# A sixth seven-product pair in the second half of an out projection

## The chip, the cores and the metric

The kernel runs on one core of a Trainium2 chip. The metric is device microseconds of one execution; times of a kernel are medians of runs on the chip. One more execution was recorded by the hardware profiler, and all rows below come from that one.

## The reference

One layer of an encoder trunk on 256 positions of width 2048, all in float32. The part that matters here is the end of the mixer:

```python
merged = g_a * (y_a @ w_branch[:GM_WIDTH]) + g_b * (y_b @ w_branch[GM_WIDTH:])
return x + merged @ w_out          # 256x2048 @ 2048x2048
```

Ahead of it stand a combined projection of the normed input, a gated MLP branch and neighbourhood attention; behind it a convolutional MLP (up projection, depthwise convolution, down projection) and a last norm.

## The kernel before, in words

**Products.** TensorE multiplies float32 with both operands split into a high and a low part, so every product of two blocks is three matmuls (`triple`, L319 to L321): high by high, low by high, high by low. Weights come from HBM in pieces of 128 rows by 1024 columns (`wraw`), and each piece is split by one ScalarE copy (`whi`, L172) and one VectorE subtraction (`wlo`, L173).

**Steps.** The whole kernel is a list of pieces; step i is TensorE's work on piece i. `begin(i)` first issues the load of piece i + 4 on SP's queue, then the split of piece i + 3, then the tasks that other code registered for step i with `at(i, f)`, in the order of their registration. So the order of every engine's queue is written out by hand, in steps. Attention's steps start at 48 (`g_at[0][1]`), the branch products of the second half of the merge at 160 (`g_m2[0][1]`), the out projection's first half (`g_o[0]`, output columns 0 to 1023) at 176, its second half (`g_o[1]`) at 192, the up projection at 208.

**Seven products.** `wide` and `run_wide` do one half of the out projection: 16 pieces, each one k block of 128 rows by two column halves of 512, against two blocks of 128 positions. A plain step is 4 products. Two neighbouring k blocks make a pair, 8 products, and a pair that is named in `OUT_QUADS` is done with 7, by sums of weight blocks and sums of activation blocks (a Winograd form). Of such a pair the first step has 3 products (into the PSUM banks P[0], C[0][0], C[0][1]) and the second has 4 (P[1], P[3], P[2], C[1][0], in that order). The four P banks run through all seven-product pairs of a half and are then added by VectorE (`ev_sums`); the four C banks hold the plain sums, and are read at the half's end (`ev_out`, L1025). `OUT_ORDER` gives the order of the k blocks: 10, 11, 0, 1, 6, 7, 2, 3, 8, 9, 4, 5 and then 12 to 15, so pair 5 comes first, then pairs 0, 3, 1, 4, 2, then two plain ones. Before, places 1 to 5 of both halves are seven-product pairs.

**Sums of weights.** For most such pairs `weight_sums` (L356 to L366, four VectorE additions) and `weight_sums_split` (L376, L377) make them close ahead of their use. For pairs 3 and 4 they are made much earlier: `split_ahead` (L1299 to L1328) is a job in attention that loads 1 MB of raw weights, makes the four additions (L1310), splits twice (ScalarE L1315, VectorE L1316) and writes four tiles of 512 KB to HBM (L1320); `split_read` (L1270) reads them back on POOL's queue into tiles of `hpool` (pair 3) or of the pool `twice` (pair 4). Of the pair's first piece only one column half is then loaded and split. `OUT_SPLIT` holds the pairs and how many steps ahead of the pair the two reads are issued. Before, the four out jobs and the four gate jobs of attention use SP's queue; out jobs load into `jobs`, most gate jobs into `jobs2`.

**Sums of activations.** `turn_m(j)` turns the merged blocks with TensorE, splits them (`split_pair`, VectorE L538) and for pairs in `OUT_PAIRS` copies them to an `f` tile on ScalarE (L982). `turned_sums` (L341) makes four sums of 128x128 from it (`act_blocks`, L325 to L328) and `act_sums_split` splits them into a tile `s0` to `s4`. `OUT_SUMS` gives the steps, counted from step 160.

**Banks.** `bank()` takes one of eight PSUM banks; a bank is handed out again when what was in it has been read.

Of the kernel before, what the change touches and what calls it, by code (L numbers as in the profile page):

```python
# [8 lines left out]
F32 = mybir.dt.float32  # L9
# [48 lines left out]
GATE_SUMS = ((0, 38, 40, "y4", "y5"), (3, 39, 40, "y6", "y7"))  # L58
GATE_LATE, Y_LATE, TURN_LATE = 7, 44, 2
KEEP_AT = (22, 25, 29)  # L60
OUT_PAIRS = (0, 1, 2, 3, 4)
OUT_SUMS = (1, 3, 6, 9, 13)
OUT_QUADS = ((1, 2, 3, 4, 5),) * 2
OUT_ORDER = ((10, 11, 0, 1, 6, 7, 2, 3, 8, 9, 4, 5, 12, 13, 14, 15),) * 2
OUT_SET = 3
OUT_JOB = (10, (15, 15, 15, 15), (17, 20))
OUT_SPLIT = ({3: (16, 14), 4: (5, 5)}, {3: (12, 10), 4: (12, 10)})
TURN_X2 = (13, 1)
Y_GAP = 224
PAD = 16  # L70
# [10 lines left out]
def trunk_kernel(ctx, tc, x, x_t, vecs, w_in, ln_g, ln_b, w_st, b_s, rpb, w_branch, w_out, w_up, w_down,  # L81
                 norm_final, out):
    nc = tc.nc
# [42 lines left out]
    raw, split_t = {}, {}  # L126
# [64 lines left out]
    def at(i, f):  # L191
        tasks.setdefault(i, []).append(f)
# [130 lines left out]
    def act_blocks(w, a11, a21, a12, a22):  # L323
        s3, n1, p2, s4 = (w[:, n * 128:(n + 1) * 128] for n in range(4))
        nc.vector.tensor_sub(s3, a11, a21)  # L325
        nc.vector.tensor_sub(n1, a22, a21)
        nc.vector.tensor_add(p2, n1, a11)
        nc.vector.tensor_sub(s4, a12, p2)  # L328
# [10 lines left out]
        box["w"] = w  # L339

    def turned_sums(q, box):  # L341
        f, w = mg["f", q], out_sums_room("f", F32)
        act_blocks(w[:, 1], *(f[:, n * 128:(n + 1) * 128] for n in range(4)))
        box["w"] = w

# [225 lines left out]
    def first_room(name, dt):  # L571
        return ypool.tile([128, 2, 512], dt, name=f"y{first_rooms.index('t13' if name == 'f' else name)}")
# [137 lines left out]
    at_pool = {}  # L710
# [193 lines left out]
    mg = {}  # L904
# [59 lines left out]

    def room_f(q):
        if ("f", q) not in mg:
            mg["f", q] = mg["fp"].tile([128, 512], F32, name=f"f{q}")
        return mg["f", q]

    def turn_m(j):  # L970
# [8 lines left out]
        for k2, p in enumerate(ps):  # L979
            k = j * 4 + k2 * 2  # L980
            if k // 2 in OUT_PAIRS:
                nc.scalar.activation(room_f(k // 2), p, AF.Copy)  # L982
# [241 lines left out]
    w_br, w_o, w_u, w_d = w_branch[0], w_out[0], w_up[0], w_down[0]  # L1224
# [3 lines left out]
    def sums_room(name, dt):  # L1228
        return s_room["p"].tile([128, 2, 512], dt, name=name)
# [15 lines left out]
    for n, (q, i, j) in enumerate(X_SUMS):  # L1245
        sum_acts_at(i, j, first_sums[2 * q], lambda q=q: q,
                    lambda name, dt, i=i: first_room("s2" if name == "f" and i < 16 else name, dt), f"s{n}", True)
    g_u = [stationary(w_in2, 0, KD, U0 + j * 512, 512, 1, 0, xt, ev_u(j)) for j in range(2)]
    def g_qk(j):
        return stationary(w_in2, 0, KD, Q0 + j * 256, 256, 2, K0 - Q0, xt, ev_qk(j))  # L1250

    def g_gate(br, j):
        return natural(w_in2, 0, KD, (GA0, GB0)[br] + j * 512, 512, xt, ev_gate(br, j))

    def g_branch(br, j):
        return natural(w_br, br * 1024, 8, j * 512, 512, lambda k: yT[br * 8 + k], ev_branch(br, j))

    g_at = [g_qk(0), g_gate(0, 0), g_qk(1), g_gate(1, 0), g_qk(2), g_gate(0, 1), g_qk(3), g_gate(1, 1),
            g_branch(0, 0), g_branch(0, 1)]
    g_m = [g_branch(1, 0), g_branch(1, 1)]  # L1260
    m_sums = {2 * q: {} for q in OUT_PAIRS}
    g_kept, x_kept = {}, {}
    gate_turn, gate_held = [0], {}

    def split_read(kept, g, tile_of, queue=nc.gpsimd):
        def read(pair, box, n):
            u = box.setdefault("u", [])
            u.append([tile_of(pair, p + n) for p in "hl"])
            for t, src in zip(u[-1], kept[pair, g][n]):
                queue.dma_start(t.bitcast(F32), src)  # L1270
            if len(u) == 2:
                split_sums(box, u)
        return read
# [20 lines left out]
    def out_sums_room(name, dt):  # L1294
        if name in ("s0", "s1", "s2", "s3"):
            return hpool.tile([128, 2, 512], dt, name=out_room[name])
        return sums_room("l24" if name == "f" else name, dt)

    def split_ahead(src, kept, room, high, queue, pair, g, c0, load_at, adds, splits, later, raw=None, last=False):  # L1299
        box = {}  # L1300

        def load():
            w = box["w"] = (at_pool[raw] if raw else room()).tile([128, 4, 512], F32, name="tw")
            ld = src.shape[-1]
            queue.dma_start(w, bass.AP(tensor=src.tensor, offset=src.offset + pair * 256 * ld + c0,
                                           ap=[[ld, 128], [128 * ld, 2], [1, 1024]]))

        def add(d, a, b):
            w = box["w"]
            nc.vector.tensor_add(w[:, d], w[:, a], w[:, b])  # L1310

        def split(c):
            w = box["w"][:, c:c + 2]
            h = box[c] = room().tile([128, 2, 512], F32R, name=high(c))
            nc.scalar.activation(h, w, AF.Copy)  # L1315
            nc.vector.tensor_sub(w.bitcast(F32R), w, h.bitcast(F32))  # L1316

        def write(c, n):
            for dst, v in zip(kept[pair, g][n], (box[c].bitcast(F32), box["w"][:, c:c + 2])):
                queue.dma_start(dst, v)  # L1320

        at(load_at, load)
        for i, (d, a, b) in zip(adds, ((0, 0, 1), (1, 1, 3), (3, 0, 3), (2, 2, 3))):
            if last:
                at(i - 1, lambda i=i, d=d, a=a, b=b: at(i, lambda: add(d, a, b)))
            else:
                at(i, lambda d=d, a=a, b=b: add(d, a, b))
        for i, c, name in zip(splits, (0, 2), ("13", "24")):  # L1328
            at(i, lambda c=c: split(c))
            at(i + later, lambda c=c, name=name: write(c, name))  # L1330

    def split_rows(name, pair, g):
        return {m: [dram.tile([128, 2, 512], F32, name=f"{name}_{h}{m}_{pair}_{g}") for h in "hl"]
                for m in ("13", "24")}

    def out_split_tile(pair, name):
        if pair == OUT_SET:
# [3 lines left out]
    t_kept = {}  # L1341
    g_o = [wide(w_o, 0, OUT_ORDER[g], g * 1024, lambda k: mg["mT"][k], OUT_QUADS[g], sums_room,
                (ev_sums(2 * g, sums_room), ev_out(g)), m_sums, split=(OUT_SPLIT[g], split_read(t_kept, g, out_split_tile)), late=g == 0) for g in range(2)]
    dram = keep("dram", space=bass.MemoryType.DRAM)
    for n, (pair, g) in enumerate((pair, g) for g in range(2) for pair in OUT_SPLIT[g]):
        t_kept[pair, g] = split_rows("out", pair, g)
        i = g_at[2 * n][1]
        split_ahead(w_o, t_kept, lambda: at_pool["jobs"], lambda c: f"th{c}", nc.sync, pair, g, g * 1024, i + OUT_JOB[0], [i + a for a in OUT_JOB[1]],
                    [i + a for a in OUT_JOB[2]], 4, last=True)
# [43 lines left out]
    sums_job(GATE_MADE[-1], g_at[8][1] + GATE_LATE, g_at[8][1] + GATE_LATE + 1, in_jobs)  # L1393
    for n, q in enumerate(OUT_PAIRS):
        i = g_m2[0][1] + OUT_SUMS[n]
        at(i, lambda n=n, q=q: turned_sums(q, m_sums[2 * q]))
        at(i + 1, lambda n=n, q=q: act_sums_split(m_sums[2 * q], out_sums_room, f"s{n}"))
# [38 lines left out]
    for p, turn in zip(DOWN_SPLIT, DOWN_JOBS):  # L1436
        for g in range(2):
            d_kept[p, g] = split_rows("down", p, g)
            i = g_up[turn[g]][1]
# [180 lines left out]
```

## Time and profile before

| what | before |
|---|---|
| median of 3 runs | 1287.13 us (1286.27 to 1287.78) |
| the profiled execution | 1286.73 us |
| its span, first to last instruction | 1285.0 us |
| TensorE busy | 1275.3 us, 99% |
| VectorE busy | 1128.1 us, 88% |
| ScalarE busy | 795.7 us, 62% |
| GpSimd (POOL) busy | 173.6 us, 14% |
| granted TensorE clock, mean | 0.999 |

A row of a timeline gives the start, the time, the engine, the line and operation, the tiles written and read, and in brackets how long the engine stood idle before it and what ended that. PE is TensorE, DVE VectorE, ACT ScalarE, POOL GpSimd, SP the queue of SyncE. A matmul's row is longer than the distance to the next one, since matmuls overlap.

### The profile page before, as it was taken

The page shows a single profiled execution, that of the slowest core. Times are in us where ns is not written, and L with a number is a line of the kernel's source. Part 1 is how long each engine was busy: PE and PEld are TensorE (multiplying, and loading weights), DVE is VectorE, ACT ScalarE, POOL GpSimd, SP SyncE. Part 2 cuts the span into 40 slices and gives each one's busy share as a digit, 9 for nine tenths or more (in the row PEclk, how much of TensorE's full clock was granted, in tenths as well). Part 3 has the DMA queues.
Part 4 walks back from the last instruction along what each step waited for, and adds up shares of the span by engine and source line. Part 5 has one row for each costly group of instructions (what it writes and reads, how often), then busy time and mean ns, then how long its engine had stood idle before and what let it go on. Part 6 is the DMA issues. An engine that isn't in the chain of part 4 may idle for free.

```text
span 1285.0 us, 19793 instructions
## 1 busy us (share of the span) xinstructions
PE 1275.3 (99%) x6711; PEld 1088.0 (85%) x6711; DVE 1128.1 (88%) x1675; ACT 795.7 (62%) x1198; POOL 173.6 (14%) x328
## 2 busy tenths in 40 slices
PE   9999999999999999999999999999999999999997
PEld 7888888888888888888888888888888888888885
DVE  7898977777799988997989999899999989989988
ACT  7776575775755555565756666566566656555554
POOL 0003752330000001100000010011001001211210
PEclk9999999999999999999999999999999999999999
DMA  9789879989789977965877888888788779999993
GB/s 368 276 273 285 292 259 346 333 287 324 253 312 366 341 248 253 395 215 180 278 239 259 297 278 251 280 286 272 249 295 294 249 254 343 353 387 333 373 385 129
DMA packets 200485, 375.54 MB, mean 292 GB/s; under 512 B 16320, under 2 KB 124480, under 8 KB 200384
## 3 DMA queue, kind: packets, MB, share of 16 engines
q1 hardware_dynamic: 175472, 285.84, 64.3%
q0 software_dynamic: 24480, 87.78, 19.4%
q8 instruction: 52, 0.85, 0.3%
q10 hardware_dynamic: 432, 0.66, 0.1%
q14 instruction: 49, 0.40, 0.1%
HBM read 323.63 MB, written 48.50 MB: 290 GB/s over the span
## 4 chain that ended last, share of the span: by engine, by line
PE 98%; DVE 1%; issue 0%; ACT 0%; DVEq 0%; ACTq 0%
PE bank L224 31%; PE bank L228 16%; PE bank L321 12%; PE bank L319 11%; PE bank L320 11%; PE bank L252 5%; PE bank L254 5%; PE bank L253 5%; DVE wlo L173 1%; PE bank L873 0%; PE bank L827 0%; PE bank L500 0%; PE bank L862 0%; PE bank L700 0%; PE bank L1052 0%; PE bank L977 0%
## 5 line engine op out<-in xcount | busy, mean ns | idle before, releaser
L173 DVE TENSOR_TENSOR wlo<-wraw,whi 128x1024 fp32r<-128x1024 f32 (+1 forms) x472 | 535.7, 1149 | 113.3 <-ACT whi L172 72.1
L172 ACT ACTIVATE whi<-wraw 128x1024 fp32r<-128x1024 f32 (+1 forms) x472 | 461.1, 993 | 218.6 <-PE bank L320 54.6
L224 PE MATMUL bank<-h,whi 128*128 128x512 f32 x1760 | 423.4, 392 | 0.0
L224 PEld LDWEIGHTS bank<-h,whi 128*128 128x128 f32 x1760 | 323.0, 188 | 61.8
L228 PEld LDWEIGHTS bank<-h,wlo 128*128 128x128 f32 x1760 | 225.9, 191 | 8.8
L228 PE MATMUL bank<-h,wlo 128*128 128x256 f32 x1760 | 228.7, 283 | 0.0
L1084 ACT ACTIVATE tc<-ta,ck 128x256 f32<-128x256 f32 x86 | 47.1, 594 | 106.4 <-DVE ta L1082 106.4
L321 PE MATMUL bank<-wlo,a 128*128 128x512 f32 x204 | 79.8, 391 | 0.2 <-DVE wlo L173 0.2
L319 PE MATMUL bank<-whi,a 128*128 128x512 f32 x204 | 79.5, 390 | 0.0
L320 PE MATMUL bank<-whi,a 128*128 128x512 f32 x204 | 79.5, 389 | 0.0
L319 PE MATMUL bank<-whi,h 128*128 128x512 f32 x168 | 66.0, 393 | 0.0
L321 PE MATMUL bank<-wlo,h 128*128 128x512 f32 x168 | 65.6, 390 | 0.0
L320 PE MATMUL bank<-whi,h 128*128 128x512 f32 x168 | 65.4, 390 | 0.0
L1087 DVE SCALAR_TENSOR_TENSOR tc<-ta,ck,tc 128x255 f32<-128x255 f32 x86 | 41.4, 482 | 14.4 <-ACT tc L1084 14.4
L376 ACT ACTIVATE h<-h 128x1024 fp32r<-128x1024 f32 x36 | 38.0, 1058 | 21.1 <-DVE h L366 17.9
L1310 DVE TENSOR_TENSOR tw<-tw 128x512 f32<-128x512 f32 x72 | 50.2, 697 | 0.7
L252 PE MATMUL bank<-whi,h 128*128 128x512 f32 x128 | 50.4, 393 | 0.0
L252 PE MATMUL bank<-whi,y 128*128 128x512 f32 x128 | 50.3, 393 | 0.0
L253 PE MATMUL bank<-whi,y 128*128 128x512 f32 x128 | 49.9, 390 | 0.0
L253 PE MATMUL bank<-whi,h 128*128 128x512 f32 x128 | 49.9, 390 | 0.0
L254 PE MATMUL bank<-wlo,h 128*128 128x512 f32 x128 | 49.9, 390 | 0.0
L254 PE MATMUL bank<-wlo,y 128*128 128x512 f32 x128 | 49.9, 390 | 0.0
(327 smaller groups left out, 1981.2 us busy)
## 6 DMA issues: line engine op xcount, KB each, us to landing
wraw<-in_w_up_dram SPq DMA_DIRECT2D x336, 256.0 KB, 4.2
wraw<-in_w_in_dram SPq DMA_DIRECT2D x107, 512.0 KB, 6.3
wraw<-in_w_down_dram SPq DMA_DIRECT2D x76, 512.0 KB, 7.6
wraw<-in_w_in_dram SPq DMA_DIRECT2D x70, 256.0 KB, 4.3
wraw<-in_w_branch_dram SPq DMA_DIRECT2D x32, 512.0 KB, 5.5
wraw<-in_w_out_dram SPq DMA_DIRECT2D x28, 512.0 KB, 6.2
tw<-in_w_down_dram POOLq DMA_DIRECT2D x10, 1024.0 KB, 8.2
down_h<-so POOLq DMA_DIRECT2D x20, 512.0 KB, 3.7
```

The lines of the kernel that those rows point to most:

```text
L172: nc.scalar.activation(h[:, k, :m], w[:, k, :m], AF.Copy)
L173: nc.vector.tensor_sub(l[:, k, :m], w[:, k, :m], h[:, k, :m].bitcast(F32))
L224: nc.tensor.matmul(p, h[:, k - k0, b * 128:(b + 1) * 128], acts(k), start=k == 0, stop=k == nk - 1)
L228: nc.tensor.matmul(p[:, :T], l[:, k - k0, b * 128:(b + 1) * 128], acts(k)[:, 0, :], start=False, stop=False)
L252: nc.tensor.matmul(p, xh, h[:, kk, :m], start=st, stop=False)
L253: nc.tensor.matmul(p, xl, h[:, kk, :m], start=False, stop=False)
L254: nc.tensor.matmul(p, xh, l[:, kk, :m], start=False, stop=sp)
L319: nc.tensor.matmul(p, xh, h, start=st, stop=False, **kw)
L320: nc.tensor.matmul(p, xl, h, start=False, stop=False, **kw)
L321: nc.tensor.matmul(p, xh, l, start=False, stop=sp, **kw)
L1084: nc.scalar.activation(v, u, AF.Identity, scale=ck[:, 1, ch:ch + 1], bias=ck[:, 3, ch:ch + 1])
L1310: nc.vector.tensor_add(w[:, d], w[:, a], w[:, b])
```

## The change

Pair 5 joins the seven-product pairs of the second half (place 0, its first two pieces). Its weight sums come from a fifth out job, the third for this half: it is put into attention at steps 56 (load), 58 and 59 (additions), 60 and 61 (splits and writes), loads into `jobs2`, and uses POOL's queue. The reads of kept sums in the second half are issued at other steps: pair 5 at 6 and 5 steps ahead of its pieces, pair 3 at 8 and 7 (before 12 and 10), pair 4 at 6 and 5 (before 12 and 10). Pair 5's activation sums are made at step 177 and split at step 178, in the first half, in a tile `s5`; they take the room of `t13`, and the `f` tile of pair 5 takes the place of pair 0's.

```diff
-OUT_PAIRS = (0, 1, 2, 3, 4)
-OUT_SUMS = (1, 3, 6, 9, 13)
-OUT_QUADS = ((1, 2, 3, 4, 5),) * 2
+OUT_PAIRS = (0, 1, 2, 3, 4, 5)
+OUT_SUMS = (1, 3, 6, 9, 13, 17)
+OUT_QUADS = ((1, 2, 3, 4, 5), (0, 1, 2, 3, 4, 5))
...
-OUT_SPLIT = ({3: (16, 14), 4: (5, 5)}, {3: (12, 10), 4: (12, 10)})
+OUT_SPLIT = ({3: (16, 14), 4: (5, 5)}, {5: (6, 5), 3: (8, 7), 4: (6, 5)})
+OUT_THIRD = (5, 1), 8, (10, 10, 11, 11), (12, 13)
...
     def turned_sums(q, box):
-        f, w = mg["f", q], out_sums_room("f", F32)
+        f, w = mg["f", q], sums_room("t13", F32) if q == 5 else out_sums_room("f", F32)
...
-            mg["f", q] = mg["fp"].tile([128, 512], F32, name=f"f{q}")
+            mg["f", q] = mg["fp"].tile([128, 512], F32, name=f"f{q % 5}")
...
-    for n, (pair, g) in enumerate((pair, g) for g in range(2) for pair in OUT_SPLIT[g]):
+    third, load_third, add_third, split_third = OUT_THIRD
+    out_jobs = [(pair, g) for g in range(2) for pair in OUT_SPLIT[g] if (pair, g) != third]
+    for n, (pair, g) in enumerate([*out_jobs, third]):
         t_kept[pair, g] = split_rows("out", pair, g)
+        if (pair, g) == third:
+            i = g_at[0][1]
+            split_ahead(w_o, t_kept, lambda: at_pool["jobs"], lambda c: f"th{c}", nc.gpsimd, pair, g, g * 1024, i + load_third,
+                        [i + a for a in add_third], [i + a for a in split_third], 0, raw="jobs2")
+            continue
```

## Rows read from the trace of the kernel before

**Rows 1.** The page: span, and TensorE's busy time, share and instructions.

```profile
span 1285.0 us, 19793 instructions
...
PE 1275.3 (99%) x6711; PEld 1088.0 (85%) x6711; DVE 1128.1 (88%) x1675; ACT 795.7 (62%) x1198; POOL 173.6 (14%) x328
```

**Rows 2.** The page: the chain that ended last, by engine.

```profile
PE 98%; DVE 1%; issue 0%; ACT 0%; DVEq 0%; ACTq 0%
```

**Rows 3.** Who waited for whom: all of TensorE's waits (total, times, longest).

```profile
PE bank L500 <- DVE one L490: 1.5, 1, 1.5
PE bank L321 <- DVE wlo L173: 0.2, 1, 0.2
```

**Rows 4.** Timeline of TensorE in the out projection.

```profile
505.50 0.39 PE L319 MATMUL bank<-h,h 128*128 128x512 f32 x1
...
506.18 0.39 PE L319 MATMUL bank<-h,h 128*128 128x512 f32 x1
...
507.54 0.39 PE L319 MATMUL bank<-h,m 128*128 128x512 f32 x1
...
519.78 0.39 PE L319 MATMUL bank<-h,s 128*128 128x512 f32 x1
...
538.14 0.39 PE L319 MATMUL bank<-whi,m 128*128 128x512 f32 x1
```

**Rows 5.** Groups by line: a job's additions and VectorE splits (busy, mean ns | idle before).

```profile
L1310 DVE TENSOR_TENSOR tw<-tw 128x512 f32<-128x512 f32 x72 | 50.2, 697 | 0.7
...
L1316 DVE TENSOR_TENSOR tw<-tw,th 128x1024 fp32r<-128x1024 f32 x16 | 19.8, 1237 | 0.0
```

**Rows 6.** Timeline of VectorE in attention: the split of piece 62.

```profile
170.20 1.23 DVE L173 TENSOR_TENSOR wlo<-wraw,whi 128x1024 fp32r<-128x1024 f32 x1 [1.44 <-ACT whi L172]
```

**Rows 7.** Timeline of TensorE: the first matmul with piece 62's low part.

```profile
179.05 0.39 PE L254 MATMUL bank<-wlo,h 128*128 128x512 f32 x1
```

**Rows 8.** Timeline of POOL in attention.

```profile
172.75 1.08 POOL L791 TENSOR_SCALAR_AFFINE_SELECT bias<-run 64x128 f32<-64x128 f32 x4 [13.96 <-DVE sc L835]
...
182.59 4.51 POOL L773 DMA_DIRECT2D run<-in_na_rpb_dram  x9
...
218.08 1.08 POOL L791 TENSOR_SCALAR_AFFINE_SELECT bias<-run 64x128 f32<-64x128 f32 x4 [25.26 <-DVE sc L835]
```

**Rows 9.** Timeline of SP's queue in attention, steps 67 and 68.

```profile
184.69 0.42 SPq L1305 DMA_DIRECT2D tw<-in_w_in_dram  x1
188.38 0.37 SPq L147 DMA_DIRECT2D wraw<-in_w_in_dram  x1
```

**Rows 10.** DMA issues by line: count, KB each, median us to landing.

```profile
out_l<-tw SPq DMA_DIRECT2D x8, 512.0 KB, 7.5
...
l<-out_l POOLq DMA_DIRECT2D x4, 512.0 KB, 14.1
```

**Rows 11.** Timeline of POOL in the out projection.

```profile
499.20 0.55 POOL L1270 DMA_DIRECT2D h<-out_h  x1
...
521.38 0.53 POOL L1270 DMA_DIRECT2D h<-out_h  x1 [5.74 <-PE bank L321]
...
524.00 0.71 POOL L1305 DMA_DIRECT2D tw<-in_w_down_dram  x1
```

**Rows 12.** Timeline of VectorE at step 177.

```profile
504.73 1.41 DVE L538 TENSOR_TENSOR m<-bank,m 128x256 fp32r<-128x256 f32 x4
506.05 1.82 DVE L173 TENSOR_TENSOR wlo<-wraw,whi 128x1024 fp32r<-128x1024 f32 x2
```

**Rows 13.** Timeline of VectorE: two of pair 4's activation sums.

```profile
491.23 0.28 DVE L325 TENSOR_TENSOR l<-f 128x128 f32<-128x128 f32 x1
491.43 0.29 DVE L326 TENSOR_TENSOR l<-f 128x128 f32<-128x128 f32 x1
```

**Rows 14.** Timeline of VectorE at the start of the second half.

```profile
539.66 2.48 DVE L1025 TENSOR_TENSOR x<-bank,x 128x512 f32<-128x512 f32 x4
```

**Rows 15.** Timeline of VectorE at the boundary of the two gate projections.

```profile
413.91 2.48 DVE L606 TENSOR_TENSOR g<-bank,g 128x512 f32<-128x512 f32 x4
```

**Rows 16.** Transfers that write or read `out_l`: us from issue to landing.

```profile
DMA to landing us min/median/max: 5.2/8.0/16.8
```

**Rows 17.** The down job's load on POOL at 524.0: us from issue to landing.

```profile
DMA to landing us min/median/max: 21.1/21.1/21.1
```

## The prediction

> **What bounds the kernel now.** I read the page's busy times first, then its chain, then what TensorE waited for, and then timelines of the three places that the change touches: attention (steps 56 to 67, about 160 to 190 us), the start of the out projection's first half (step 176) and the start of its second half (step 192, 538.14 us [rows 4]). The reader is to see an engine that is never short of work: TensorE is busy for 1275.3 of 1285.0 us [rows 1], it makes up 98% of the chain that ended last [rows 2], and over the whole span it waited twice for another engine, 1.7 us together [rows 3]. So a matmul taken out is worth its spacing, work taken off another engine is worth nothing, and the change can lose only where it makes TensorE wait.
>
> The spacing isn't the 0.39 us that a matmul's row shows, since matmuls overlap: from 505.50 to 507.54 nine of them start, one every 0.227 us [rows 4]. A plain step, twelve matmuls, is 2.72 us.
>
> **What is removed.** In the second half pair 5 (k blocks 10 and 11, first in the order) goes from eight products to seven. A product is three matmuls, so three of 128x512 go: 3 x 0.227 = **0.68 us off** the only engine on the path. Of piece 192 one column half is loaded and split in place of two, which saves VectorE and ScalarE about half an instruction each. TensorE waits for neither there [rows 3], so I count that at nothing.
>
> **What is added, and what hides it.**
>
> (a) The third job in attention: four additions of 128x512 at 0.697 us and two splits at 1.237 us [rows 5], 5.3 us of VectorE in steps 58 to 61; ScalarE has the two copies of the splits, by the same row some 2.5 us. It is hidden by the lead of the split weights: the low part of piece 62 ends at 171.43 [rows 6] and its first matmul runs at 179.05 [rows 7], 7.6 us later. All of the 5.3 us in one place would leave 2.3 us, and VectorE has gaps there too (1.44 us idle before 170.20 [rows 6]). Cost zero. Without that cover it would be up to 5.3 us.
>
> (b) The job's five POOL instructions: a 1 MB load at step 56 and two writes each at steps 60 and 61. They stand ahead of the loads for attention's next bias block. POOL now sits idle for 13.96 us until 172.75, fills the time to 182.59 with the second block's masks, and waits 25.26 us, until 218.08, for the scores that use them [rows 8]. The writes can go only after the splits, at about 178 and 182. Behind them come 16 bias loads, some 8 us by the pace of the nine in [rows 8], their landing (I allow 5 to 6 us) and 10 us of masks: done by about 206, some 12 us early. Cost zero.
>
> (c) SP: the gate job's load at 184.69 [rows 9] goes into the space that the third job's low parts are written out from, so it now waits until they have landed, and the weight loads behind it wait too. Writes issued at about 182 land by about 190 (7.5 us in the median [rows 10]). SP's next load stands at 188.38 as it is [rows 9], so 1 to 2 us is passed on to weights that are split 7 us ahead. Cost zero.
>
> (d) The reads. Pair 5's four reads of 512 KB join POOL at steps 186 and 187, when the first half has finished with the `twice` tiles (about 521.4, where pair 4's reads wait now [rows 11]). They are needed nine matmuls into the second half, from 540.2 on. Pair 3 follows. Pair 4 goes behind step 193, to about 543, and is used from step 201 on: four pairs of 21 matmuls and nine more after 538.14, at 559.2. The first down job's load, at 524.00 now [rows 11], moves behind them all; its additions come at step 214, in the next stage. By the median 14.1 us of such reads [rows 10] all are in time, the last with 2 us. Cost zero.
>
> (e) The activation sums of pair 5. ScalarE copies one more block in `turn_m(2)`; VectorE makes four 128x128 instructions at step 177 and a split at 178. **This is the one place where I expect a price.** At step 177 they stand in VectorE's queue ahead of the four instructions that empty the two banks of `turn_m(3)`, from 504.73 to 506.14 [rows 12]. In the program as built, the products P[3] and P[2] of the first seven-product pair use just these banks. P[3] starts at 506.18 [rows 4] and P[2] three matmuls later, at 506.86; the banks come free at about 505.45 (after two of the four) and 506.14. Four of the new instructions at 0.28 us [rows 13] are 1.1 us, and those rows show VectorE starting a new instruction where the last one ends, with no gap to take them. The banks then come free at about 506.55 and 507.25, and P[3] waits 506.55 - 506.18 = some **0.4 us**; P[2], moved by as much, has its bank. Bounds: nothing (VectorE reaches that point 0.4 us earlier) and 1.1 us (the two banks change places). I take 0.4, since it comes from the rows of this very place. The weights that follow lose 1.1 us of lead and the split's 0.7, of which 3 to 4 us are there by the same kind of row; TensorE doesn't notice.
>
> (f) Eight PSUM banks at once at step 192. Now four are taken there and four two steps later. The first half's C sums are read out by four instructions from 539.66 to 542.14 [rows 14], after the second half has begun. Handed out in the order of release, as the program does now, the four idle P banks come first, and the fifth is needed after 12 matmuls, at 540.86, against its release some 0.68 us after 539.66, at 540.35. The gate projections do the same at their boundary (four reads from 413.91 to 416.39 [rows 15]), and no wait stands there [rows 3]. Cost zero, with 0.5 us of lead; bounds nothing and the rival below.
>
> **The sum.** -0.68 + 0.4 = -0.28 us. The profiled execution took 1286.73 us, so it would become 1286.45. The median of the runs is 1287.13, 0.40 above the profiled one and inside their spread of 1.5 us, so I forecast a median of 1286.9.
>
> **Rivals.**
>
> *No wait at all.* If VectorE is 0.4 us early at step 177, the gain is the full 0.68: 1286.45. For it: TensorE hardly ever waits. Against: VectorE's queue shows no gap there.
>
> *The old C banks come first at step 192.* Then the first product waits for 540.35: 2.2 us. With (e): -0.68 + 0.4 + 2.2 = +1.9, 1289.0. Against it stands the gate boundary [rows 15].
>
> *Pair 4's first-half reads come late.* The pool `sums` grows by a tile (`s5`), so `twice` above it moves into space that the `f` tiles held. The four reads issued from 499.20 on [rows 11] would in part wait until pair 5's sums are made, to about 506. By the median 14.1 us [rows 10] they land at 520 to 521, about when step 185 needs them (519.78 [rows 4]); by the longest, 16.8 us [rows 16], the last lands at 507 + 16.8 = 523.8, and TensorE, which wants it six matmuls into the step, at 521.5 with the wait of (e), stands for 2.3 us: +2.0, 1289.1. Against it: fewer transfers are queued ahead of them than ahead of the present ones.
>
> *Slower: the third job's load lands late.* VectorE works in order, and the job's first additions stand ahead of the low part of piece 62. The load is issued, at the latest, when step 56 begins and the gMLP tiles under its buffer are done, six steps before 179.05, at about 162. If it lands at L, piece 62 is ready at about L + 2.5 (two additions and its split), so the point from which it decides is L = 176.5, 14.5 us after issue. A load of this size on POOL took 21.1 us once [rows 17]. At 162 + 21.1 = 183.1 TensorE waits 6.5 us, and the queue behind is late by some 2 us more: +8.5 - 0.3, 1295.3. Against it: that load had the reads of [rows 11] queued ahead of it.
>
> Beside this stands a rule that speaks against the change. The Trainium skill (SBUF — State Buffer, "SBUF: two separate sides") says that a DMA issued from GpSimd has its descriptors written by that engine, which certain VectorE instructions lock out, and that an SP or ACT queue avoids it. By that rule the third job, on POOL where the other jobs of attention are on SP, is the one to suffer, and the time would be this rival's. The trace doesn't bear it out so far: POOL's issue at 499.20 takes 0.55 us [rows 11], while VectorE runs without a gap.
>
> **How the numbers follow.** About 0.2%, 2.6 us, is what a measurement of this kernel can tell from no change. Chances: forecast 0.50; no wait 0.20; C banks first 0.08; late reads 0.10; late load 0.07; the rest 0.05, split between an unforeseen wait over 0.2% (0.02) and a gain over 0.2% (0.03), which no row offers, since only 1.7 us of waits exist. The first four lie within 0.2%: 0.88. Slower 0.09, faster 0.03. The range goes from the no-wait case less some of the runs' scatter, 1285.6, to just above the cases at 1289; it leaves out the late load and the rest.
>
> **What would show each step right or wrong.** Right: three matmuls fewer; a wait of TensorE near 506.2 of about 0.4 us for VectorE's L538, and none at step 192, at step 185 or in attention; the second block's masks done before 214. Wrong: a wait at L254 near 179 (the load), at the first product of step 192 (banks), or for a read at step 185, 193 or 201; or a time more than 2.6 us from 1287.1.

## The result, and the profile after

| what | before | after |
|---|---|---|
| median, 22 runs each on the same chip | 1287.01 us (1286.27 to 1288.48) | 1289.41 us (1287.78 to 1290.90) |
| ratio | 1 | 1.0018, interval 1.0012 to 1.0024 |
| span of the profiled execution | 1285.0 us | 1288.1 us |

The change costs 2.4 us. That is 0.18%, less than the 0.2% that the prediction took for the least that can be told from no change; with 22 runs each the interval leaves 1 out, so the loss is real. The sign is not the one that was forecast, and the median lies above the range, which ended just above 1289.

The page of the changed kernel, span and busy times, to be held against [rows 1]:

```profile
span 1288.1 us, 19813 instructions
...
PE 1276.1 (99%) x6708; PEld 1086.9 (84%) x6708; DVE 1134.3 (88%) x1686; ACT 797.9 (62%) x1202; POOL 188.6 (15%) x337
```

Three matmuls are gone, as they should. What replaced them stands in the view of who waited for whom (total, times, longest), all of TensorE's waits, to be held against [rows 3]:

```profile
PE bank L501 <- DVE one L491: 1.5, 1, 1.5
PE bank L322 <- DVE wlo L174: 0.8, 1, 0.8
PE bank L320 <- DVE m L539: 0.6, 1, 0.6
PE bank L320 <- DVE x L1026: 0.6, 1, 0.6
PE bank L1053 <- DVE x L1026: 0.5, 1, 0.5
```

The first was there before. (Line numbers of these functions are one higher than before; runs whose edit adds lines shift them again, so that L1028 below is this L1026.) Three new ones are waits for a PSUM bank that VectorE has yet to read: the bank of the last turned block (L539), the first half's C bank at the start of the second half (L1026), and the second half's C bank at the start of the up projection (L1026 again). The second row, at 1270 us at the end of the kernel, is the same wait as the 0.2 us of [rows 3]; it came out between nothing and 1.5 us in the profiles of these runs, with and without the change, so I take no part of it for the change.

To see what the out projection alone costs, two points of TensorE are enough: the matmul after the transposes at 480.7 us, well ahead of everything new in the merge, and the one after the transposes for the row norm at 604.5 us. Timelines of TensorE, first the kernel before, then the changed one:

```profile
480.71 0.48 PE L252 MATMUL bank<-whi,y 128*128 128x512 f32 x1
...
604.47 3.89 PE L224 MATMUL bank<-h,whi 128*128 128x512 f32 x16
```

```profile
480.84 0.48 PE L253 MATMUL bank<-whi,y 128*128 128x512 f32 x1
...
506.09 0.39 PE L322 MATMUL bank<-l,h 128*128 128x512 f32 x1
507.08 0.47 PE L320 MATMUL bank<-h,h 128*128 128x512 f32 x1 [0.60 <-DVE m L539]
...
541.65 0.39 PE L322 MATMUL bank<-l,s 128*128 128x512 f32 x1
542.60 0.50 PE L320 MATMUL bank<-h,s 128*128 128x512 f32 x1 [0.57 <-DVE x L1026]
...
571.11 0.39 PE L322 MATMUL bank<-wlo,m 128*128 128x512 f32 x1
571.57 1.25 PE L1053 MATMUL bank<-ident,x 128*128 128x128 f32 x8
...
583.56 0.27 PE L1053 MATMUL bank<-ident,x 128*128 128x128 f32 x1
584.35 0.87 PE L1053 MATMUL bank<-ident,x 128*128 128x128 f32 x6 [0.52 <-DVE x L1026]
...
606.90 1.40 PE L225 MATMUL bank<-h,whi 128*128 128x512 f32 x5
```

From the first point to the second: 123.76 us before, 126.06 after, **+2.30 us**. I call this stretch **S** below; it leaves out the first microseconds and the end of the kernel, where profiles of one kernel differ by some tenths. Matmuls start 0.23 us apart, so the gaps are 0.76 us too long at 506, 0.72 at 541 and 0.69 at 583 (the transposes there usually start 0.1 us apart). After each wait the next matmuls are a little further apart too (507.08 to 507.39), so that, matmul by matmul against the kernel before, 0.88 us is lost at 506, 0.90 at 541 and 0.73 at 583. At 571, where transposes begin, another 0.47 us is lost in small steps (the first of them starts 0.46 us after the matmul ahead of it). Sum: -0.68 + 0.88 + 0.90 + 0.47 + 0.73 = +2.3.

Why the first two banks come late is in the timelines of VectorE and POOL of the changed kernel:

```profile
504.86 0.28 DVE L326 TENSOR_TENSOR t<-f 128x128 f32<-128x128 f32 x1
...
505.71 0.29 DVE L329 TENSOR_TENSOR t<-f,t 128x128 f32<-128x128 f32 x1
506.18 1.42 DVE L539 TENSOR_TENSOR m<-bank,m 128x256 fp32r<-128x256 f32 x4 [0.18 <-DMA x<-in_x_dram]
...
519.90 0.69 DVE L367 TENSOR_TENSOR t<-wraw 128x512 f32<-128x512 f32 x1 [0.54 <-DMA wraw<-in_w_out_dram]
...
541.86 2.48 DVE L1026 TENSOR_TENSOR x<-bank,x 128x512 f32<-128x512 f32 x4
```

```profile
499.29 0.57 POOL L1271 DMA_DIRECT2D h<-out_h  x1
506.56 0.55 POOL L1271 DMA_DIRECT2D l<-out_l  x1 [6.70 <-DVE t L329]
...
546.22 0.70 POOL L1306 DMA_DIRECT2D tw<-in_w_down_dram  x1
```

The reader is to see three things. The four sums stand ahead of L539, as forecast. L1026 starts at 541.86, where it started at 539.66 [rows 14]. And POOL's second read of pair 4, issued at 499.74 before, waits 6.70 us for the last of the new sums (L329), since its tile lies where pair 5's `f` tile still is; the two reads behind it wait too, and two residual loads behind these (loads of `x`, which went out at 513.12 before) go out at 508.15. The first down job's load has moved from 524.00 [rows 11] to 546.22.

### The profile page after: what moved, and what is told of

Read it like the earlier page. It is cut to its first block, busy times and chain, and to the rows that moved or that the text cites. A ratio compares the mean times of both kernels' runs of the same rounds, so it can differ in the third digit from the quotient of the medians.

```text
span 1288.1 us, 19813 instructions
## 1 busy us (share of the span) xinstructions
PE 1276.1 (99%) x6708; PEld 1086.9 (84%) x6708; DVE 1134.3 (88%) x1686; ACT 797.9 (62%) x1202; POOL 188.6 (15%) x337
## 4 chain that ended last, share of the span: by engine, by line
PE 52%; DVE 1%; DMA 1%; issue 0%; DVEq 0%; ACT 0%; SPq 0%; ACTq 0%
PE bank L225 24%; PE bank L229 13%; PE bank L322 5%; PE bank L321 5%; PE bank L320 5%; DMA wraw<-in_w_down_dram 1%; DVE wlo L174 1%; PE bank L1053 0%; DVE h L367 0%; DVE h L378 0%; DVE h L1001 0%; DVEq L1623 0%; DVE x L1199 0%; DVE h L363 0%; DVE x L1026 0%
## 5 line engine op out<-in xcount | busy, mean ns | idle before, releaser
L174 DVE TENSOR_TENSOR wlo<-wraw,whi 128x1024 fp32r<-128x1024 f32 (+1 forms) x472 | 535.5, 1148 | 109.4 <-ACT whi L173 75.5
L1311 DVE TENSOR_TENSOR tw<-tw 128x512 f32<-128x512 f32 x76 | 53.5, 704 | 0.7
```

What stands on the lines that cost most here:

```text
L174: nc.vector.tensor_sub(l[:, k, :m], w[:, k, :m], h[:, k, :m].bitcast(F32))
```

## The experiments

Of each: the edit, what was expected, the median beside that of the kernel before on the same chip, and S as its difference to the kernel before (from the same two points of each profile). S is the sharper measure, though it comes from one profile of each kernel; the intervals of the ratios are about 0.09% to either side, 1.2 us.

### The job in attention alone (e1)

```diff
-OUT_PAIRS = (0, 1, 2, 3, 4, 5)
+OUT_PAIRS = (0, 1, 2, 3, 4)
-OUT_QUADS = ((1, 2, 3, 4, 5), (0, 1, 2, 3, 4, 5))
+OUT_QUADS = ((1, 2, 3, 4, 5),) * 2
-..., {5: (6, 5), 3: (8, 7), 4: (6, 5)})
+..., {3: (12, 10), 4: (12, 10)})
```

> The kernel before, with the third job of attention added (its load, four additions, two splits and four writes on POOL's queue), and nothing that uses it. Theory: the changed kernel's 2.4 us are lost in the out projection alone, so this one takes the time of the kernel before, 1287.0 within 0.5, and its TensorE has no new wait in attention. Rival (the job costs something by itself, through the weights split behind it or the gate job's load): 1287.8 or more, with a wait of TensorE between 160 and 260 us.

1287.20 against 1286.67, ratio 1.0005 (0.9996 to 1.0014); S +0.00. TensorE's only wait is that of L501. What the median is above (0.5 us) cannot be told from nothing, and the profile has TensorE at the down projection 0.35 us later than before, 0.10 of it from the first microseconds and 0.25 from about 415 us, at the boundary of the gate projections; none of it between 160 and 260 us. The job is free.

### Pair 3's reads bunched, in the kernel before (e2)

```diff
-OUT_SPLIT = (..., {3: (12, 10), 4: (12, 10)})
+OUT_SPLIT = (..., {3: (8, 7), 4: (12, 10)})
```

> The kernel before, with pair 3's four reads of the second half issued 8 and 7 steps ahead in place of 12 and 10, as the changed kernel does. Theory (reads that are issued together with the weights of steps 191 to 195 make these land late, and VectorE with them): the four reads at about 522 to 527 stretch the weight loads issued from 523 to 531 and the first half's last bank reads (L1025, 539.66 in the kernel before) start about 1 us later or more; TensorE doesn't wait there, since before the change the banks are wanted some 5 us later; time 1287.0 to 1287.6. Rival (the lateness comes from the sixth pair's own work, not from the traffic): L1025 starts at 539.7 within 0.3.

1286.69 against 1286.67, ratio 1.0001 (0.9992 to 1.0009); S +0.00. VectorE's row:

```profile
539.39 2.48 DVE L1025 TENSOR_TENSOR x<-bank,x 128x512 f32<-128x512 f32 x4
```

Not late at all: my first theory, that the reads bunched at 522 to 527 make the weights late, failed here.

### Pair 3's reads early, in the changed kernel (e4)

```diff
-OUT_SPLIT = (..., {5: (6, 5), 3: (8, 7), 4: (6, 5)})
+OUT_SPLIT = (..., {5: (6, 5), 3: (12, 10), 4: (6, 5)})
```

> The changed kernel, with pair 3's reads of the second half issued 12 and 10 steps ahead, as before the change, in place of 8 and 7. Theory: four of the eight reads of 522 to 527 leave that window, the weights of pieces 193 to 196 land some 2 us earlier, L1026 starts by 540.5 in place of 541.86, and TensorE's wait at 541.65 (0.6 us) goes: 1288.6 within 0.4; the waits at 571 and 583 stay or shrink. Rival (eight banks taken at once at step 192 make TensorE wait for the old C bank, whatever VectorE is late by): the wait near 541 stays at 0.5 or more and the time at 1289.4 within 0.3.

1288.23 against 1286.67, ratio 1.0013 (1.0005 to 1.0022); S +2.51, and the waits are those of the changed kernel, with one more of 0.3 us (L1053, for VectorE's L999); L1026 starts at 542.22.

A second miss for the theory. The rival, eight banks, had its wait, but the next runs show the same eight banks without it.

### Pair 5's reads left out (e7)

```diff
+            if (pair, g) == OUT_THIRD[0]:
+                u.append(held_four[n])
+            else:
...
+                if pair == 4:
+                    held_four[n] = u[-1]
```

> The changed kernel without the four reads of pair 5: its products use the tiles that pair 4 of the first half read, so the products are those of other weights; TensorE, VectorE and ScalarE do the same work. 2 MB less moves between 522 and 535. Theory (too many bytes from 510 to 558): weight loads of 526 to 530 land in 8 to 9 us in place of 8.5 to 11.9, L1026 starts by 541, the wait at 541 shrinks below 0.2 and those at 571 and 583 by half or more: 1288.0 within 0.5. Rival (VectorE's own delay, from step 177, decides): the wait at 541 stays at 0.5 or more; time 1289.0 or more.

1289.57 against 1287.13, ratio 1.0019 (1.0010 to 1.0029); S +2.52. Rows of VectorE, and of the weight loads issued from 525.4 to 531 (count, KB, median us to landing):

```profile
542.29 2.48 DVE L1026 TENSOR_TENSOR x<-bank,x 128x512 f32<-128x512 f32 x4
```

```profile
wraw<-in_w_out_dram SPq DMA_DIRECT2D x3, 512.0 KB, 5.3
```

With 2 MB fewer the loads there land in 5.3 us, not 9.8 as in the changed kernel, and L1026 is as late as ever. So pair 5's reads don't decide; VectorE is late from somewhere earlier.

### The sums three steps earlier (e3)

```diff
-OUT_SUMS = (1, 3, 6, 9, 13, 17)
+OUT_SUMS = (1, 3, 6, 9, 13, 14)
...
-        f, w = mg["f", q], sums_room("t13", F32) if q == 5 else out_sums_room("f", F32)
+        f, w = mg["f", q], out_sums_room("f", F32)
```

> The changed kernel, with pair 5's activation sums made at step 174 and split at 175, in the room that pair 4's sums use, in place of steps 177 and 178. Theory: the wait for the banks of the last turned block at 506 us (0.8 us with its aftermath) is these four instructions standing ahead of L539; it goes, and the waits near 541, 571 and 583 stay: 1288.6 within 0.4. Rival (VectorE has no gap before step 177, so that the same 1.1 us arrive there anyway): the wait stays at 0.6 and the time at 1289.4.

1287.64 against 1286.67, ratio 1.0007 (0.9998 to 1.0016); S +0.60. More was gained than the wait at 506: the one at 541 went too. VectorE:

```profile
540.60 2.48 DVE L1026 TENSOR_TENSOR x<-bank,x 128x512 f32<-128x512 f32 x4
```

In their place TensorE waits at 500 for VectorE's L954, some 0.76 us in all: here the sums stand ahead of the merged blocks that `turn_m(3)` turns. But the edit does two things. It moves 1.8 us of VectorE's work, and it sets pair 5's `f` tile free before POOL comes to its reads (the second one is now issued at 500.31). The next two runs take these apart, from both sides.

### The sums early, the reads held (e5)

```diff
+    at(g_m2[0][1] + 17, lambda: nc.vector.tensor_copy(junk[:, :8], mg["f", 5][:, :8]))
```

> The early sums of e3, with one more reader of pair 5's f tile: a VectorE copy of 128x8 at step 177, behind the sums' old place, so that POOL's reads of pair 4 for the first half, and the residual loads behind them, wait until about 506 again. What tells apart what e3 took away. Theory (the place of the 1.8 us on VectorE decides): no wait at 541 and a time of 1287.7 within 0.4, as e3. Rival (the reads held until 506.56 push the transfers of 508 to 520, and with them the weights, VectorE and the bank reads at 541): L1026 starts at 541.5 or later, the wait at 541 is back with 0.5 or more, and the time is 1288.5 or more.

1289.12 against 1287.13, ratio 1.0014 (1.0005 to 1.0022); S +2.04. POOL and VectorE:

```profile
506.80 0.55 POOL L1271 DMA_DIRECT2D l<-out_l  x1 [6.91 <-DVE junk L1406]
```

```profile
541.76 2.48 DVE L1026 TENSOR_TENSOR x<-bank,x 128x512 f32<-128x512 f32 x4
```

The rival was right: a copy of 128x8 that does nothing but hold the reads brings the wait at 541 back (0.51 us for L1026), with sums that are long done.

### The sums at step 177, the reads not held (e11)

```diff
-        if ("f", q) not in mg:
+        if ("f", q) not in mg and q == 5:
+            mg["f", q] = sums_room("s5", F32)[:, 1]
+        elif ("f", q) not in mg:
```

> The changed kernel, with pair 5's f tile in the room of s5, the sums left at step 177. What tells the two causes apart, with e5 from the other side. Theory: the wait at 506 stays at 0.6 (0.85 with its aftermath), the four reads of pair 4 are issued by 503 and the wait at 541 goes: 1288.3 within 0.5. Rival (the 1.8 us of sums on VectorE make the wait at 541 too): it stays at 0.5 or more, 1289.2 or more.

1287.94 against 1286.98, ratio 1.0007 (0.9998 to 1.0016); S +1.36. VectorE and TensorE:

```profile
540.73 2.48 DVE L1028 TENSOR_TENSOR x<-bank,x 128x512 f32<-128x512 f32 x4
```

```profile
541.82 0.39 PE L322 MATMUL bank<-l,s 128*128 128x512 f32 x1
542.04 0.39 PE L320 MATMUL bank<-h,s 128*128 128x512 f32 x1
```

The wait at 506 stays and the one at 541 is gone: P[3] of step 193 starts 0.22 us after the matmul ahead of it. So the held reads make that wait, and 0.9 us of S with it (2.30 - 1.36). How they do it is read from rows. First the weight loads issued from 508 to 517. Rows of the kernel before, of the changed one, of this run and of the one with the reads held, in this order:

```profile
wraw<-in_w_out_dram SPq DMA_DIRECT2D x4, 512.0 KB, 7.1
```

```profile
wraw<-in_w_out_dram SPq DMA_DIRECT2D x4, 512.0 KB, 8.3
```

```profile
wraw<-in_w_out_dram SPq DMA_DIRECT2D x4, 512.0 KB, 6.5
```

```profile
wraw<-in_w_out_dram SPq DMA_DIRECT2D x4, 512.0 KB, 8.9
```

Held until 506.6, the reads and residual loads meet the weights of the first half; VectorE then waits for weights: in the changed kernel 0.54 us at 519.90, as shown. The gaps near 518 to 520 stand in the profiles with the reads held (1.01 and 0.53 us with the sums early) and not in those of e3, e11 and the kernel before; e2, e9 and e10 have one of 0.2 to 0.4 us. VectorE waits for weights again just ahead of the bank reads, 0.67, 0.80 and 0.42 us from 535.5 to 539.9, but so it does in this run (0.70, 0.80 and 0.26) and in e3 (0.65 and 1.06), where TensorE doesn't wait at 541: these gaps don't tell the kernels apart.

### The reads held, in the kernel before (e12, e13)

Two runs. The first put a GpSimd copy from the last turned block ahead of the reads:

```diff
+    held = const.tile([128, 8], F32, name="held")
+    at(g_m2[0][1] + 18, lambda: nc.gpsimd.tensor_copy(held, mg["mT"][15][:, 1, :8].bitcast(F32)))
```

> The kernel before, with its first-half reads of pair 4 and all that POOL issues behind them held as in the changed kernel: a GpSimd copy of 128x8 from the last turned block (written at about 506 us) stands ahead of them. No sixth pair, no job. What the hold does by itself. Theory (the held reads meet the weight loads of 508 to 521 and make VectorE late; only where eight banks are wanted at once does TensorE wait for it): the reads are issued at about 506 to 508, L1025 starts 1 us or more after 539.66, TensorE has no wait at 541, since the kernel before needs these banks some 5 us later, and the time stays within 0.4 of the kernel before. Rival (the hold alone doesn't make VectorE late; it takes the sums' 1.8 us as well): L1025 starts by 540.0. Rival (the hold costs TensorE time by itself, by reads that come late for step 185): a wait near 521 and 1287.5 or more.

1297.10 against 1286.85, ratio 1.0078 (1.0065 to 1.0092). It held more than the change does: the first two residual loads, which stand ahead of the reads, and the first read too. The reads were issued from 511.60 on and landed from 521.08 to 528.76, and TensorE stood for them at step 185, for 0.32, 1.36 and 1.83 us. TensorE's timeline of the last of these waits, and stretches of the run (us, busy PE, PEld, DVE, ACT, POOL, then the granted clock, share and GB/s of the DMAs):

```profile
528.80 0.80 PE L321 MATMUL bank<-l,s 128*128 128x512 f32 x1 [1.83 <-DMA l<-out_l]
529.40 0.63 PE L319 MATMUL bank<-h,m 128*128 128x512 f32 x1
529.83 0.63 PE L320 MATMUL bank<-h,m 128*128 128x512 f32 x1
```

```profile
526.00:530.00 4.00, 1.93 (x5) 1.30 (x6) 2.15 (x2) 0.71 (x1) 1.06 (x2) 0.74 1.03 410
530.00:535.00 5.00, 5.00 (x14) 3.90 (x13) 1.23 (x1) 1.73 (x2) 1.06 (x2) 0.53 1.02 402
```

This is the rival of late reads, which the change escaped, and more than its price of 2.0 us: behind the waits stands a clock at its lower level. (3.0 us of the 10 were lost before the hold; see the last section.) About the question it says nothing. The second run holds the three reads that the change holds, and no tile moves:

```diff
-    const.tile([128, PAD], F32, name="pad")
+    spare = const.tile([128, PAD], F32, name="pad")
...
+                if (pair, g) == (4, 0) and kept is t_kept and len(u) == 1 and t is u[0][0]:
+                    nc.gpsimd.tensor_copy(spare[:, :8], mg["mT"][15][:, 1, :8].bitcast(F32))
```

> The kernel before, with pair 4's second to fourth reads for the first half held as in the changed kernel: a GpSimd copy of 128x8 from the last turned block, behind the first read, into a spare tile that is there already, so that no other tile moves (e12's new tile moved others by 32 bytes, and its copy stood ahead of the residual loads too). No sixth pair, no sums at step 177. Theory (held reads meet the weight loads of 508 to 517 and make VectorE late; only where eight banks are wanted at once does TensorE wait for it): the second read is issued between 505.5 and 508, the four weight loads of 508 to 517 land in 8 us or more in the median in place of 7.1, L1025 starts 0.6 to 1.6 us after 539.66, TensorE waits neither at 521 nor at 541, and the time is that of the kernel before within 0.5. Rival (VectorE absorbs the hold when the sums don't stand at step 177): L1025 starts by 540.0. Rival (the hold costs TensorE time by itself): a new wait of 0.3 us or more and 1287.5 or more.

1287.11 against 1286.60, ratio 1.0004 (0.9995 to 1.0013); S +0.00. The second read goes out at 508.25. The loads of 508 to 517, and VectorE:

```profile
wraw<-in_w_out_dram SPq DMA_DIRECT2D x5, 512.0 KB, 8.1
```

```profile
541.26 2.47 DVE L1025 TENSOR_TENSOR x<-bank,x 128x512 f32<-128x512 f32 x4
```

This profile runs 0.99 us behind that of the kernel before at 501 us already (and at 604), so L1025, 1.60 us later, is 0.6 us late beside TensorE. Without a hold, e1 and e2 have it 0.1 us late and 0.5 us early by the same reckoning, so 0.6 is a small effect in one profile. TensorE doesn't wait: this kernel wants the bank two steps later.

### The sums on GpSimd (e8)

```diff
-OUT_SUMS = (1, 3, 6, 9, 13, 17)
+OUT_SUMS = (1, 3, 6, 9, 13, 14)
...
+        act_blocks(..., on=nc.gpsimd if q == 5 else None)
```

The room of the sums is that of the run with the sums three steps earlier.

> The changed kernel, with the four sums of pair 5 made by GpSimd at step 174 in place of VectorE at step 177 (the split at step 175 stays on VectorE). Theory (VectorE has no room for these 1.1 us anywhere between 490 and 510): no wait at 500 (e3 had 0.5 to 0.8 there), 506 or 541: 1287.0 within 0.5. Rival (the gain of e3 came from the earlier release of f5 and its room alone, and GpSimd's slower sums push the reads back): the time lies above e3's 1287.6.

1289.32 against 1287.13, ratio 1.0017 (1.0008 to 1.0026); S +2.05. Worse than with the sums on VectorE. TensorE, POOL, VectorE:

```profile
501.30 0.33 PE L979 MATMUL bank<-ident,g 128*128 128x128 f32 x1 [1.07 <-DVE g L955]
```

```profile
495.38 0.94 POOL L328 TENSOR_TENSOR l<-f 128x128 f32<-128x128 f32 x1
```

```profile
496.80 0.95 DVE L368 TENSOR_TENSOR t<-wraw 128x512 f32<-128x512 f32 x1
498.76 0.69 DVE L352 TENSOR_TENSOR s<-l,s 128x512 fp32r<-128x512 f32 x1 [1.01 <-ACT s L351]
```

GpSimd's sums end at about 498.0; the split of these sums (L352, and L351 on ScalarE ahead of it) waits for them in VectorE's queue, and the merged blocks that TensorE wants (L955) stand behind it. Work taken off an engine came back as a wait on the same engine. The rival's reason was not the one: the reads go out from 500.05 to 502.14, hardly held, and no wait at 541 is listed.

### The down job's load later (e6)

```diff
-            queue.dma_start(w, ...)
+            (first or queue).dma_start(w, ...)
...
+                        first=nc.sync if (p, g) == (DOWN_SPLIT[0], 0) else None)
```

> The changed kernel, with the load of the first down job (1 MB, POOL at 546.2) on SP's queue at step 208, some 15 us later. Theory (this load and pair 4's reads make the weights of steps 200 to 207 land late, VectorE's last bank reads with them): weight loads of 548 to 554 land in 6 to 7 us in place of 8 to 9.5, the waits at 571 and 583 (1.2 us with their aftermath) go, those at 506 and 541 stay: 1288.2 within 0.4. Rival (VectorE simply carries its delay of 541 through the half): both waits stay, 1289.4 within 0.3.

1288.65 against 1287.13, ratio 1.0013 (1.0004 to 1.0021); S +1.99. The weight loads issued from 546 to 555, of the kernel before, the changed one and this one:

```profile
wraw<-in_w_out_dram SPq DMA_DIRECT2D x5, 512.0 KB, 4.8
```

```profile
wraw<-in_w_out_dram SPq DMA_DIRECT2D x4, 512.0 KB, 8.5
```

```profile
wraw<-in_w_out_dram SPq DMA_DIRECT2D x4, 512.0 KB, 6.0
```

The waits at 571 and 583 are gone, 1.2 us. That at 541 (1.43 us listed) happened to be 0.9 us longer, though the program doesn't differ up to there, which hides most of the gain in S; in the five profiles of the changed kernel and its variants with the reads held this wait came out between 0.51 and 1.43 us.

### The repairs together (e9, e10)

The `f` tile apart, with `OUT_SUMS = (1, 3, 6, 9, 13, 25)`: the sums at step 185.

> The changed kernel, with pair 5's f tile in the room of s5 (so that the reads of pair 4 for the first half need not wait for pair 5's sums), and the sums made at step 185 and split at 186, where VectorE of the kernel before stood idle for 2.5 us between 524 and 528. Theory (two causes: the order on VectorE at step 177, and the reads held until 506.56): no wait at 500 or 506, POOL's four reads of pair 4 issued by 503, the wait at 541 gone or below 0.2, that of 583 (VectorE late through the down job's load) left with 0.5 to 0.8: 1287.0 within 0.4. Rival (VectorE is short by these 1.8 us wherever they stand): a wait at 541 of 0.5 or more, 1288 or more.

1286.88 against 1286.98, ratio 0.9999 (0.9990 to 1.0008); S -0.48. VectorE:

```profile
523.88 0.28 DVE L326 TENSOR_TENSOR t<-s 128x128 f32<-128x128 f32 x1
...
539.54 2.48 DVE L1028 TENSOR_TENSOR x<-bank,x 128x512 f32<-128x512 f32 x4
```

No new wait is listed. P[3] starts at 541.20 on a bank whose read began at 539.54. In the waiting runs TensorE starts 0.74 us after that (542.60 - 541.86), so 541.20 - 539.54 - 0.74 = 0.92 us of lead are left. With the down job's load late as well:

> As e9, and the first down job's load on SP's queue at step 208, as in e6. Theory: with the order on VectorE, the held reads and the late weights of the half's end all taken away, what is left is the three matmuls that the change saves: TensorE has no new wait anywhere, 1286.3 within 0.4, some 0.7 below the kernel before of the same chip. Rival (some wait only moves): a wait of 0.5 or more between 540 and 590, 1287.0 or more.

1286.75 against 1286.98, ratio 0.9998 (0.9989 to 1.0007); S **-0.68**, the three matmuls and nothing else:

```profile
481.24 0.48 PE L253 MATMUL bank<-whi,y 128*128 128x512 f32 x1
...
604.32 3.89 PE L225 MATMUL bank<-h,whi 128*128 128x512 f32 x16
```

All profiles but e12's, whose hold was another, can be set side by side: from TensorE's first matmul of step 192 to the start of the bank reads (538.14 to 539.66 in the kernel before, 1.52 us). In the eight whose reads were not held until 506 (before, e1, e2, e3, e8, e9, e10, e11) it is 1.05 to 1.88 us, in the six with held reads (after, e4, e5, e6, e7, e13) 2.13 to 3.57. P[3] follows twelve matmuls, 2.72 us, after that first one, so with 0.74 us from the start of the reads TensorE stands wherever it is more than 1.98 and eight banks are wanted. The weight loads of 508 to 517 land in 6.5 to 8.0 us in the eight and in 8.1 to 8.9 in the six: the same order, but hardly a gap between, so that the way from the hold to VectorE through the weights is likely and not shown by a run of its own.

The theory holds: the order on VectorE at step 177 makes the wait at 506, the held reads that at 541, and behind these two the moved load makes the losses at 571 and 583. That this version is faster than the kernel before is seen in S of one profile and in the direction of the median, but a difference of 0.2 us is not resolved by these runs.

## Why the prediction was wrong

**What was right.** The gain: three matmuls, 0.68 us, and with every new wait taken away S fell by just that. The place of the wait of (e). Parts (a) to (c): the job in attention costs nothing (S +0.00). The rival of a late load had its point of decision at 176.5 us; the load was issued at 155.97 and landed in 9.9 us. The job of the same size on SP's queue, in the same stretch of the changed kernel, took 10.0:

```profile
tw<-in_w_out_dram POOLq DMA_DIRECT2D x1, 1024.0 KB, 9.9
tw<-in_w_out_dram SPq DMA_DIRECT2D x1, 1024.0 KB, 10.0
```

The rule that stood beside that rival (the Trainium skill, SBUF — State Buffer, "SBUF: two separate sides") is about VectorE instructions in a mode that takes the port pair shared with GpSimd, and would have made POOL's load the slower of the two; these rows show no such delay. VectorE's rows beside this load (155.97 to 166) are all TENSOR_TENSOR, and the rows try the rule on no other instruction.

**Where it failed.** The forecast was -0.28 us, S is +2.30. The 2.58 us between them are 0.48 at 506 (0.88 in place of 0.4), 0.90 at 541, and 0.47 and 0.73 at 571 and 583, which were put at nothing. The steps:

- *Part (d) and its rival.* That POOL's reads would be held to about 506 was foreseen, and only one question was asked of it: do they come in time for step 185? They did (landed by 515.4). What was not asked is what they meet when they go out 7 us later: the weight loads of 508 to 517, then VectorE, then the bank at 541. The price is 0.9 us of S by the one run (2.30 - 1.36) and 1.4 by the other (2.04 - 0.60); by the medians beside their kernel before it is 1.4 (2.40 - 0.96) and 1.0 (1.99 - 0.97). The Trainium skill states the link (DMA: Bandwidth & Descriptors, "Issuing engines are not separate DMA queues"): transfers issued from different engines run on the same 16 DMA engines and interleave. The rows agree, by a small margin: SP's loads take 8.1 to 8.9 us in the median with the reads held on POOL, 6.5 to 8.0 without.
- *Part (e), the last sentence,* "the weights that follow lose 1.1 us of lead and the split's 0.7 [...] TensorE doesn't notice". A lead was counted for weights only. The time that VectorE loses also makes late what else stands in its queue, and the bank reads had no 3 us. With the sums at step 185 L1028 starts at 539.54, with the sums at 177 at 540.73; 0.84 us of this is TensorE's own delay from 506, so beside TensorE it is 0.35 us later, of 0.92 us of lead: too little for a wait at 541 by itself. S is +1.36 in place of -0.48. Of these 1.84 us the wait at 506 is half; the rest stands at 571 and 583, and how it comes there from the sums was not followed.
- *Part (e), the 0.4 us.* The mechanism was right and the size off: 0.88, or 0.76 without what follows the wait. The four sums plus the step to L539 take 1.32 us (504.86 to 506.18), not 1.1: the last two need the result ahead of them and start 0.32 and 0.33 us after it, where the first two start 0.20 us apart, and VectorE is idle for 0.18 us ahead of L539. And P[3] starts 0.90 us after L539, not 0.72.
- *Part (d), "the first down job's load [...] moves behind them all".* It was asked when it is needed, not what it meets: the weights of 546 to 555 took 8.5 us, and 6.0 with that load elsewhere. The waits at 571 and 583 go without it (1.2 us), but it does not make them alone: in the run with the sums at step 185 and the reads not held the load is still at 544.67, and only some 0.2 us is left at 581.
- *Part (f)* was right as far as it went. The bank's lead was given as 0.5 us; it is 0.92 in e9 and e10, whose sums and reads are out of the way. But it was taken as a property of the order of banks, while it depends on all that VectorE does in the 35 us ahead of it: 0.57 with the sums at 177 (e11), and -0.67 to -1.59 us in the five profiles of the changed kernel and its variants with the reads held.

The rival of a wait at step 192 had almost the measured time, 1289.0, for another reason (old C banks handed out first, which no row shows), and the range was built on it; that the range nearly reached the measured time is luck. Each mishap was taken by itself, and three came together.

What stays open: why the wait at 541 differed by 0.9 us between two profiles of the same instructions up to there, by which way the held reads make VectorE late, and whether the last version is faster than the kernel before in its median.

## What to carry to other kernels

A tile that is freed later delays not only its own readers: ask of every transfer that moves which other transfers it now meets, and who waits for those. Where a resource begins to be wanted without slack (here eight PSUM banks at once), a lateness of the engine that frees it beyond the little lead that is left turns into a wait, though the same lateness was free before; so sum up over its whole queue what the change makes late, not part by part. A small work item that must run on a full engine goes where that engine waits for data, and its input goes to a place that nobody else wants meanwhile.

## What the runs showed of the hardware

- The position of tiles seems to matter. The `held` tile of the first holding run (e12) is 32 bytes per partition; by the kernel's pools (`const` and the weights on one side, the `y` tiles on the other) the weight pieces behind it lie 32 bytes further, the `y` tiles do not. The same matmuls of one branch product and its transposes, from 458.06 to 480.71 us in the kernel before (22.65 us), take from 459.94 to 483.23 there (23.29 us), 2.8% longer, with no wait and at a granted clock of 1.00. In the 14 other profiles it is 22.65 or 22.66 us, in that of the second holding run too, which has the copy and no new tile. TensorE was 3.0 us behind at 505 us, ahead of the copy at 509. That the 32 bytes do it is inferred: no run moved the tiles alone.
- The clock. In that run TensorE was busy for 1.93 of 4.00 us from 526 to 530; from 530 to 535 the granted clock is 0.53, the lower of its two levels (1.2 GHz), and matmuls start 0.43 us apart (529.40, 529.83) in place of 0.23. From 535 on it is 1.00 again.
- In e8 GpSimd needs 0.46 to 0.94 us for a sum of 128x128 for which VectorE takes 0.28 [rows 13], and VectorE's additions of 128x512 beside it took 0.95 us in place of 0.69.
